# Hybrid attention and convolution block on one core: weighing V for four row tiles at once

## The chip, the cores and the metric

The kernel runs on one core of one Trainium2 chip. The metric is the device time of one execution in microseconds; lower is better. TensorE (PE) multiplies and transposes, VectorE (DVE) and ScalarE (ACT) work elementwise, GpSimd (POOL) clears small pieces of memory and issues a few DMAs, and SyncE (SP) issues nearly all DMAs.

## The reference

One layer: a normed input is projected to q, k, v, u and g; differential attention and a convolution branch run beside each other, are gated, merged and projected, and a SwiGLU follows. The change is in the attention alone (1024 tokens, 8 heads, v of 128 columns):

```python
def probs(qb, kf):
    s = jnp.einsum('bhqd,bhkd->bhqk', qb, kf) * scale + bias
    s = jnp.where(causal, s, -jnp.inf)
    return jax.nn.softmax(s, axis=-1)

p = probs(qb1, k1f) - lamf * probs(qb2, k2f)
return jnp.einsum('bhqk,bhkd->bhqd', p, vf)
...
a = rms_norm(a, subln_w[l]) * (1.0 - lam_init)
y_a = a.reshape(B, S, ATTN_WIDTH) @ w_proj_attn[l]
```

All of it is float32. Query row i sees keys up to i, so of the 8 x 8 tiles of 128 x 128 probabilities of a head, 36 are not zero.

## The kernel before, in words

Every float32 product is computed as three products of rounded parts (`mm3`, lines 171 to 173): high by high, high by low, low by high. `split_hi` (line 138, ScalarE) and `split_lo` (line 143, VectorE) make the parts.

The attention stage is a loop over 64 steps: 8 heads times 8 row tiles of 128 queries. Between its own matmuls stand those of the input projection that are still to be done (q, k and gate columns for later heads, tile `pg`), as filler for TensorE, and the taps of the depthwise convolution as filler for VectorE (tile `acc`, line 652).

For row tile i of head h a step does this:

- `scores(h, i)`: two score matmuls for each of the two softmaxes and each piece of up to 512 keys (tile `sc`, lines 1193 and 1194); VectorE adds the bias and finds the row bound (line 1195), ScalarE takes the exponential (line 1200), and VectorE joins both softmaxes into one unnormalised row (line 1209).
- `turn` of the step before: TensorE transposes its i + 1 probability tiles (`pT`, line 1229), and the two splits write them into `ph` and `pl`. These two tiles have one buffer each, with 8 key tiles of 256 query columns. So two row tiles fill one pair of tiles, the even one in columns 0 to 127, the odd one in 128 to 255. The even row tile has one key tile fewer than the odd one, and this hole is cleared by GpSimd (lines 1219 and 1220).
- `weigh`, after each odd row tile, in the same step as its `turn`: for each key tile up to the odd one's, three matmuls with a 128 x 128 tile of V as weights and 256 columns of `ph` or `pl` moving, all into one PSUM bank `pW`. With b = 0 to 3 these are 2, 4, 6 and 8 key tiles, 60 matmuls per head. ScalarE copies the result to `ar` (line 1243).
- `back`, two steps later: two transposes of `ar` (`pB`, line 1249), and for each row tile two ScalarE activations, one that scales and one that squares and sums (lines 1257 and 1258).
- After the last `back` of a head, `subln` scales its rows, and one step later `subln_T` transposes them (`pS`, line 1270), writes two tiles `at` (line 1272) and stores them in DRAM.

V of a head (`vh`, `vl`, one buffer each) is loaded after the last `weigh` of the head before.

`slot` runs what is due of `backs`, the late transposes of q and k (`pQ`, line 863), `sublns` and `weighs`, in this order and behind the projection work of the step. `slack_of` estimates how much longer TensorE takes than VectorE in each step, and the convolution's taps are dealt out by it. Three PSUM banks serve `pT`, `pW`, `pB`, `pS` and `pQ` in turn, three the scores, and two the projection. Within what the program fixes, the framework orders the instructions of each engine when the kernel is built, by a model of their times.

Of the kernel before, what the change touches and what calls it, by code (L numbers as in the profile page):

```python
# [10 lines left out]
F32 = mybir.dt.float32  # L11
F32R = mybir.dt.float32r
# [4 lines left out]
P = 128  # L17
S = 1024
D = 1024
H = 8  # L20
# [11 lines left out]
NT = S // P  # L32
# [43 lines left out]
def kernel(  # L76
# [28 lines left out]
    dve, act, pool, pe = nc.vector, nc.scalar, nc.gpsimd, nc.tensor  # L105
# [24 lines left out]
    def nm(s):  # L130
        uid[0] += 1
        return f"{s}_{uid[0]}"

    def f32(ap):
        return ap.bitcast(F32)

    def split_hi(dst, src):
        act.copy(dst, src)  # L138

    last_lo, last_mm = [None], [None]  # L140

    def split_lo(dst, src, hi):
        last_lo[0] = dve.tensor_tensor(dst, src, f32(hi), op=ALU.subtract).ins  # L143

    def after(ins):

        return nullcontext() if ins is None else tc.issue_after(ins)

    def last_of(engine):
        for ins in reversed(nc.cur_bb.bb.instructions):  # L150
            if ins.engine == engine:
                return ins
# [12 lines left out]
    def pm(z="pm"):  # L165
        npm[0] += 1
        p_, tag = pms[npm[0] % len(pms)]
        return p_.tile([P, 512], F32, tag=tag, name=nm(z))

    def mm3(o, lh, ll, rh, rl, start, stop):  # L170
        pe.matmul(o, lh, rh, start=start, stop=False)  # L171
        pe.matmul(o, lh, rl, start=False, stop=False)  # L172
        last_mm[0] = pe.matmul(o, ll, rh, start=False, stop=stop).ins  # L173
# [67 lines left out]
    at = [0]  # L241
# [884 lines left out]
    n = 0  # L1126
# [25 lines left out]
    aps = at_ctx.enter_context(tc.tile_pool(name="attn", bufs=2, reuse_waits="tile"))  # L1152
# [4 lines left out]
    V, TB, AN, SSA, PT, ES, RL = {}, {}, {}, {}, {}, {}, {}  # L1157

    def load_v(h):
        vh = aps.tile([P, NT, VD], F32R, tag="vh", name=f"vh{h}", bufs=1)  # L1160
        vl = aps.tile([P, NT, VD], F32R, tag="vl", name=f"vl{h}", bufs=1)
        for dst, src in ((vh, v_hi[h // 4]), (vl, v_lo[h // 4])):
            nc.sync.dma_start(
                f32(dst[:]),
                src[:, (h % 4) * VD : (h % 4 + 1) * VD].rearrange("(k p) d -> p k d", p=P),
            )
        V[h] = vh, vl

    def load_bias(h):
        tb = aps.tile([P, S], F32, tag="tb", name=f"tb{h}", bufs=1)  # L1170
        skew = t_d[h][:].rearrange("p l -> (p l)")[P - 1 : P - 1 + P * (TL - 1)]
        nc.sync.dma_start(tb[:], skew.rearrange("(p l) -> p l", l=TL - 1)[:, :S])
        TB[h] = tb

    def scores(h, i):
# [34 lines left out]
        dve.reciprocal(RL[h][:, i : i + 1], l[:, 0:1])  # L1210
        ES[h, i] = E[0]

    def turn(h, i):

        b = i // 2
        if (h, b) not in PT:
            ph = aps.tile([P, NT, 256], F32R, tag="ph", name=nm("ph"), bufs=1)
            pl = aps.tile([P, NT, 256], F32R, tag="pl", name=nm("pl"), bufs=1)
            pool.memset(f32(ph[:, 2 * b + 1, 0:P]), 0.0)
            pool.memset(f32(pl[:, 2 * b + 1, 0:P]), 0.0)  # L1220
            PT[h, b] = ph, pl
        ph, pl = PT[h, b]
        e = ES.pop((h, i))
        qs = slice((i % 2) * P, (i % 2 + 1) * P)
        for k0 in range(0, i + 1, 4):
            n = min(4, i + 1 - k0)
            pt = pm("pT")
            for k in range(n):
                pe.transpose(pt[:, k * P : (k + 1) * P], e[:, (k0 + k) * P : (k0 + k + 1) * P], ident[:])  # L1229
            src = pt[:, : n * P].rearrange("p (k q) -> p k q", q=P)  # L1230
            split_hi(ph[:, k0 : k0 + n, qs], src)
            split_lo(pl[:, k0 : k0 + n, qs], src, ph[:, k0 : k0 + n, qs])

    def weigh(h, b):

        ph, pl = PT.pop((h, b))
        vh, vl = V[h]
        o = pm("pW")
        nkt = 2 * b + 2
        for k in range(nkt):  # L1240
            mm3(o[:, :256], vh[:, k, :], vl[:, k, :], ph[:, k, :], pl[:, k, :], k == 0, k == nkt - 1)
        ar = aps.tile([P, 256], F32, tag="ar", name=nm("ar"), bufs=1)
        act.copy(ar[:], o[:, :256])
        return ar

    def back(h, b, ar):
        pt = pm("pB")
        for e in range(2):
            pe.transpose(pt[:, e * P : (e + 1) * P], ar[:, e * P : (e + 1) * P], ident[:])
        if h not in AN:  # L1250
            AN[h] = aps.tile([P, NT, VD], F32, tag="an", name=f"an{h}", bufs=1)
            SSA[h] = sm.tile([P, NT], F32, tag="ssa", name=nm("ssa"))
        jk = sm.tile([P, VD], F32, tag="jk", name=nm("jk"), bufs=1)
        for e in range(2):
            i = 2 * b + e
            src, r = pt[:, e * P : (e + 1) * P], RL[h][:, i : i + 1]
            act.activation(AN[h][:, i, :], src, AF.Identity, scale=r)
            act.activation(jk[:], src, AF.Square, scale=r, accum_out=SSA[h][:, i : i + 1])

    def subln(h):  # L1260
        an = AN[h]
        r = rstd_of(SSA[h][:], NT, 1.0 / VD, fast=True)
        dve.tensor_tensor(an[:], an[:], r.unsqueeze(2).to_broadcast([P, NT, VD]), op=ALU.mult)

    def subln_T(h):
        an = AN[h]
        for sb in range(2):
            pt = pm("pS")
            for i in range(4):
                pe.transpose(pt[:, i * P : (i + 1) * P], an[:, 4 * sb + i, :], ident[:])  # L1270
            at = aps.tile([P, 512], F32, tag="at", name=nm("at"), bufs=2)
            act.activation(at[:], pt[:], AF.Identity, scale=pcol("subln"))
            nc.sync.dma_start(a_d[h][:, sb * 512 : (sb + 1) * 512], at[:])
# [9 lines left out]
    scm, weighs, backs, sublns = [], [], [], []  # L1283
# [3 lines left out]
    def more(k):  # L1287

        with after(scm[-4] if len(scm) >= 4 else None):
            for _ in range(k):  # L1290
                next(fill, None)
        last_fill[0] = last_mm[0]
# [3 lines left out]
    def ready(queue, n):  # L1296
        now = [e for e in queue if e[0] <= n]
        queue[:] = [e for e in queue if e[0] > n]
        return [e[1] for e in now]

    def slot(n, nq):

        with after(last_fill[0]):
            for h, b, ar in ready(backs, n):
                back(h, b, ar)
                if b == NT // 2 - 1:
                    subln(h)
                    sublns.append((n + 1, h))
            for _ in range(nq):
                if late[0][0] <= n:  # L1310
                    late.pop(0)[1]()
            for h in ready(sublns, n):
                subln_T(h)
            for h, b in ready(weighs, n):
                backs.append((n + 2, (h, b, weigh(h, b))))
                if b == NT // 2 - 1 and h + 1 < H:
                    load_v(h + 1)

    def slack_of(h, i):

        p = (i + 1) * plan[h] // NT - i * plan[h] // NT
        nk = (i + 1) * P
        t_pe = nk * (2.52e-3 + (2.5e-3 if i % 2 else 0.0)) + 5.15 * p
        t_dve = 0.4 + 4.2e-3 * nk + p + 0.3
        return max(0.0, t_pe - t_dve)

# [5 lines left out]
    for n, (h, i) in enumerate(steps):  # L1332
        if i == 0:
            load_bias(h)
        p = (i + 1) * plan[h] // NT - i * plan[h] // NT
        nq = len(late)
        scores(h, i)
        scm.append(last_mm[0])
        more((p + 1) // 2)
        if n:  # L1340
            hp, ip = steps[n - 1]
            turn(hp, ip)
            if ip % 2:
                weighs.append((n, (hp, ip // 2)))
        more(p // 2)
        slot(n, nq)
        due += share * slack[n]
        with after(last_of(mybir.EngineType.DVE)):
            bg.step(int(due + 1e-6))
        due -= int(due + 1e-6)  # L1350
# [19 lines left out]
    def behind(*engines):  # L1370

        st = ExitStack()
        for e_ in engines:
            st.enter_context(after(last_of(e_)))
        return st

    hl, bl = H - 1, NT // 2 - 1
    with behind(E_.PE, E_.Activation, E_.DVE):
        wg = ws.next()
        with in_order(E_.PE):  # L1380
# [1 line left out]
    with after(last_mm[0]):  # L1382
        for h, b, ar in ready(backs, len(steps)):
            back(h, b, ar)
        ar = weigh(hl, bl)
# [40 lines left out]
    for h in KB:  # L1426
        for sb in range(2):
            cs = slice(sb * 512, (sb + 1) * 512)
            at = bp.tile([P, 512], F32, tag="ya", name=f"at{h}_{sb}", bufs=4)[:]
# [230 lines left out]
    o, part_ = {}, {}  # L1660
# [16 lines left out]
    for z, (a_, b_, s_, outs) in enumerate(YO):  # L1677
        start = s_ not in o
# [133 lines left out]
    o = {}  # L1812
    for z, (a_, b_, s_, (l, c), full) in enumerate(WO):
        if z == 6:
            h2_hi, h2_lo = Quad(big, "h2_hi", "xh"), Quad(big, "h2_lo", "xl")
        start = s_ not in o
        if start:
            o[s_] = [(pw if s_ == "c" else ps).tile([P, 512], F32, tag="pw" if s_ == "c" else PS_TAGS[i], name=nm("wo")) for i in range(4)]
        with in_order(mybir.EngineType.PE):
            for g in range(2):  # L1820
# [3 lines left out]
                for i in range(4):  # L1824
                    for k in range(2):
                        ah, al = a_part(a_, 2 * g + k, i)
                        for y_, (l_, r_) in enumerate(((ah, whi), (ah, wlo), (al, whi))):
                            last_mm[0] = pe.matmul(  # L1828
                                o[s_][i][:], l_, r_[:, k, :], start=start and g + k + y_ == 0,
                                stop=g == 1 and k == 1 and y_ == 2, skip_group_check=not start,  # L1830
# [3 lines left out]
        with in_order(mybir.EngineType.DVE, alone=True) if z == 5 else nullcontext():  # L1834
# [3 lines left out]
            for i in range(4):  # L1838
                t_ = 4 * l + i
                h = xa[t_][:, TOK[c]]  # L1840
# [322 lines left out]
```

## Time and profile before

| | |
|---|---|
| Median of 3 runs | 1722.73 us (1722.38 to 1724.52) |
| The profiled execution, time | 1722.03 us |
| Its span | 1720.0 us |
| Granted TensorE clock, mean | 1.0 |
| Attention stage, about | 320 to 825 us |
| Weighing matmuls (`pW`) | 480, first at 341.7 us, last at 817.7 us |

The profile gives the busy time of each engine, groups of instructions by line and shape, and single instructions with their start and duration. A row of the latter reads: start in us, duration in us, engine, line, operation, what is written from what, shape, count, and in brackets how long the engine had been idle and what released it. `PE` is the matmul itself, `PEld` the load of its weights, which runs beside other matmuls. The ends of matmuls are modelled; their starts are recorded.

### The profile page before, as it was taken

How to read it: one execution, taken by the hardware profiler on the slowest of the kernel's cores; microseconds unless marked ns; L12 is line 12 of the kernel's file. 1: busy time of each engine (PE TensorE's matmuls, PEld its weight loads, DVE VectorE, ACT ScalarE, POOL GpSimd, SP SyncE). 2: the span in 40 equal slices, each digit the busy share in tenths (PEclk: the TensorE clock that was granted, in tenths of full speed). 3: DMA queues.
4: the chain of work that ended last, by engine and by line, in shares of the span. 5: the costliest groups of instructions: out<-in, count | busy, mean ns of one | idle time of the engine just before them, and what ended most of it. 6: DMA issues, size and time to landing. Idle time of an engine off the chain costs nothing.

```text
span 1720.0 us, 25299 instructions
## 1 busy us (share of the span) xinstructions
PE 1711.1 (99%) x8882; PEld 1458.3 (85%) x8882; DVE 1334.0 (78%) x2275; ACT 822.5 (48%) x1926; POOL 27.2 (2%) x101
## 2 busy tenths in 40 slices
PE   9999999999999999999999999999999999999999
PEld 6878898999989998988888888888888888888887
DVE  8689988989988898987589797867776777555544
ACT  6121141558767686665557444853333333333332
POOL 0000000000000000000000000000000000000000
PEclk9999999999999999999999999999999999999999
DMA  7269544244444344355899565476756656687663
GB/s 246 87 202 314 183 127 127 70 123 129 112 125 131 116 117 132 108 147 163 295 323 321 183 238 199 159 246 208 227 188 206 189 184 191 203 287 241 216 215 128
DMA packets 286362, 318.57 MB, mean 185 GB/s; under 512 B 19106, under 2 KB 186067, under 8 KB 286236
## 3 DMA queue, kind: packets, MB, share of 16 engines
q1 hardware_dynamic: 283500, 307.07, 55.6%
q0 software_dynamic: 2432, 9.10, 2.2%
q8 instruction: 70, 1.15, 0.3%
q10 hardware_dynamic: 304, 0.79, 0.1%
q14 instruction: 56, 0.46, 0.1%
HBM read 204.91 MB, written 97.82 MB: 176 GB/s over the span
## 4 chain that ended last, share of the span: by engine, by line
PE 93%; DMA 2%; DVE 2%; ACT 2%; issue 0%; SPq 0%; ACTq 0%; DVEq 0%
PE acc L1875 20%; PE acc L578 12%; PE pg L171 12%; PE pg L172 12%; PE pg L173 11%; PE wo L1828 4%; PE yo L1671 4%; PE pg L779 4%; PE eg L1875 2%; PE sc L1194 2%; PE sc L1193 2%; PE pT L1229 2%; PE pW L171 1%; PE pW L173 1%; PE pW L172 1%; PE pQ L863 1%
## 5 line engine op out<-in xcount | busy, mean ns | idle before, releaser
L652 DVE SCALAR_TENSOR_TENSOR acc<-u,cw,acc 128x1024 f32<-128x1024 f32 x240 | 306.8, 1278 | 2.6
L171 PE MATMUL pg<-hT_hi,whi 128*128 128x512 f32 x512 | 201.7, 394 | 1.2 <-ACT sgg L688 0.9
L172 PE MATMUL pg<-hT_lo,whi 128*128 128x512 f32 x512 | 201.1, 393 | 0.0
L173 PE MATMUL pg<-hT_hi,wlo 128*128 128x512 f32 x512 | 200.8, 392 | 0.0
L138 ACT CAST whi<-wraw 128x1024 fp32r<-128x1024 f32 x106 | 111.7, 1053 | 158.4 <-PE pg L172 90.1
L143 DVE TENSOR_TENSOR wlo<-draw,whi 128x1024 fp32r<-128x1024 f32 x75 | 91.8, 1224 | 93.5 <-ACT whi L138 93.5
L143 DVE TENSOR_TENSOR wlo<-wraw,whi 128x1024 fp32r<-128x1024 f32 x107 | 130.5, 1220 | 42.3 <-ACT whi L138 41.8
L171 PE MATMUL pg<-whi,hT_hi 128*128 128x256 f32 x512 | 146.1, 285 | 0.3 <-ACT jk L847 0.3
L172 PE MATMUL pg<-wlo,hT_hi 128*128 128x256 f32 x512 | 145.7, 285 | 0.0
L173 PE MATMUL pg<-whi,hT_lo 128*128 128x256 f32 x512 | 145.3, 284 | 0.0
L138 ACT CAST whi<-draw 128x1024 fp32r<-128x1024 f32 x75 | 79.1, 1055 | 129.5 <-PE acc L578 126.0
L578 PE MATMUL acc<-wlo,whi 128*128 128x512 f32 x308 | 119.8, 389 | 0.0
L578 PE MATMUL acc<-whi,wlo 128*128 128x512 f32 x308 | 119.8, 389 | 0.0
L1200 ACT ACTIVATE E<-E,mn 128x256 f32<-128x256 f32 (+7 forms) x128 | 99.4, 778 | 33.0 <-DVE mn L1195 32.8
L171 PEld LDWEIGHTS pg<-hT_hi,whi 128*128 128x128 f32 x512 | 96.2, 188 | 21.3 <-ACT sgg L688 1.7
L172 PEld LDWEIGHTS pg<-hT_lo,whi 128*128 128x128 f32 x512 | 96.2, 188 | 19.3 <-issue 0.6
L173 PEld LDWEIGHTS pg<-hT_hi,wlo 128*128 128x128 f32 x512 | 96.2, 188 | 19.2
L171 PEld LDWEIGHTS pg<-whi,hT_hi 128*128 128x128 f32 x512 | 97.6, 191 | 1.9 <-ACT jk L847 0.5
L172 PEld LDWEIGHTS pg<-wlo,hT_hi 128*128 128x128 f32 x512 | 97.6, 191 | 1.5
L173 PEld LDWEIGHTS pg<-whi,hT_lo 128*128 128x128 f32 x512 | 97.6, 191 | 0.7
L1195 DVE CUSTOM_DVE_ANT_0 E<-sc,tb 128x512 f32<-128x512 f32 (+3 forms) x128 | 73.9, 586 | 17.3 <-PE sc L1194 6.3
L138 ACT CAST whi<-s 128x1024 fp32r<-128x1024 f32 x44 | 46.3, 1053 | 81.3 <-PE acc L1875 67.6
(392 smaller groups left out, 4285.8 us busy)
## 6 DMA issues: line engine op xcount, KB each, us to landing
wraw<-in_w_gate_up_dram SPq DMA_DIRECT2D x55, 512.0 KB, 5.7
wraw<-in_w_in_dram SPq DMA_DIRECT2D x37, 512.0 KB, 5.6
qs<-qs SPq DMA_DIRECT2D x96, 128.0 KB, 2.3
wd<-in_w_down_dram SPq DMA_DIRECT2D x44, 256.0 KB, 3.4
tdT<-wd SPq DMA_DIRECT2D x88, 128.0 KB, 4.2
draw<-sdS SPq DMA_DIRECT2D x44, 256.0 KB
draw<-tdT SPq DMA_DIRECT2D x44, 256.0 KB, 3.0
wraw<-in_w_in_dram SPq DMA_DIRECT2D x32, 256.0 KB, 4.6
```

The costliest lines, as they stand in the source:

```text
L138: act.copy(dst, src)
L143: last_lo[0] = dve.tensor_tensor(dst, src, f32(hi), op=ALU.subtract).ins
L171: pe.matmul(o, lh, rh, start=start, stop=False)
L172: pe.matmul(o, lh, rl, start=False, stop=False)
L173: last_mm[0] = pe.matmul(o, ll, rh, start=False, stop=stop).ins
L578: m = pe.matmul(o[s_][i][:], l_[:, ts], r_[:, 512:], start=start and j + y_ == 0, stop=j == n - 1 and y_ == 2, skip_group_check=not start,)
L652: dve.scalar_tensor_tensor(acc[0][:], us[c][:, t : t + S], cw[:, c, t : t + 1], acc[0][:], op0=ALU.mult, op1=ALU.add)
L779: last_mm[0] = pe.matmul(o[:], l_, r_, start=first and n_ == 0, stop=last and n_ == len(terms) - 1).ins
L1195: dve.tensor_tensor_reduce(e[:, ks], o[:, :w], tb[:, S - nk + c0 : S - nk + c0 + w], 1.0, mn[:, j : j + 1] if c0 else 3.0e38, ALU.add, ALU ...
L1200: act.activation(e[:, :nk], e[:, :nk], AF.Exp, bias=mn[:, j : j + 1], scale=-1.0, accum_out=l[:, j : j + 1])
L1671: last_mm[0] = pe.matmul(ob_[0][j][:], l_[:, j % 2, k, :], r_, start=start and k + y_ == 0, stop=k == 3 and y_ == 2, skip_group_check=not ...
L1875: last_mm[0] = pe.matmul(o[:], a_[x_][:, k, :], b_[y_][:, k, :], start=start and k + x_ + y_ == 0, stop=k == 3 and x_ == 1, skip_group_che ...
```

## The change

Row tiles 0 to 3 of a head become one group, which is weighed once, after row tile 3. Row tiles 4 and 5, and 6 and 7, stay pairs. The buffer of `ph` and of `pl` keeps its 2048 columns and is read as 4 key tiles of 512 query columns for the first group, and as 8 of 256 for the pairs. In the first group key tile k is multiplied only with the columns from 128 k on, since earlier queries don't see it: 512, 384, 256 and 128 columns. Nothing has to be cleared there. The low by high product of key tile 0 is moved to the end, so that the last matmul covers the whole bank. `ar` gets 512 columns and shares the two buffers of `at`. `back` turns four row tiles back together for the first group. The estimate in `slack_of` is adapted.

```diff
+    GROUPS = ((0, 4), (4, 2), (6, 2))
+
+    def group_of(i):
+        return max(0, i // 2 - 1)
+
     def turn(h, i):
 
-        b = i // 2
+        b = group_of(i)
+        q0, nq = GROUPS[b]
         if (h, b) not in PT:
-            ph = aps.tile([P, NT, 256], F32R, tag="ph", name=nm("ph"), bufs=1)
-            pl = aps.tile([P, NT, 256], F32R, tag="pl", name=nm("pl"), bufs=1)
-            pool.memset(f32(ph[:, 2 * b + 1, 0:P]), 0.0)
-            pool.memset(f32(pl[:, 2 * b + 1, 0:P]), 0.0)
-            PT[h, b] = ph, pl
+            PT[h, b] = [
+                aps.tile([P, NT * 256], F32R, tag=t_, name=nm(t_), bufs=1)[:].rearrange("p (k q) -> p k q", q=nq * P)
+                for t_ in ("ph", "pl")
+            ]
+            if b:
+                for t_ in PT[h, b]:
+                    pool.memset(f32(t_[:, q0 + 1, 0:P]), 0.0)
         ph, pl = PT[h, b]
         e = ES.pop((h, i))
-        qs = slice((i % 2) * P, (i % 2 + 1) * P)
+        qs = slice((i - q0) * P, (i - q0 + 1) * P)
...
         o = pm("pW")
-        nkt = 2 * b + 2
-        for k in range(nkt):
-            mm3(o[:, :256], vh[:, k, :], vl[:, k, :], ph[:, k, :], pl[:, k, :], k == 0, k == nkt - 1)
-        ar = aps.tile([P, 256], F32, tag="ar", name=nm("ar"), bufs=1)
-        act.copy(ar[:], o[:, :256])
+        q0, nq = GROUPS[b]
+        terms = [
+            (l_[:, k, :], r_[:, k, c0:], c0)
+            for k in range(q0 + nq) for c0 in [0 if b else k * P] for l_, r_ in ((vh, ph), (vh, pl), (vl, ph))
+        ]
+        if not b:
+            terms.append(terms.pop(2))
+        for n_, (l_, r_, c0) in enumerate(terms):
+            last_mm[0] = pe.matmul(
+                o[:, c0 : nq * P], l_, r_, start=n_ == 0, stop=n_ == len(terms) - 1, skip_group_check=c0 > 0
+            ).ins
+        ar = aps.tile([P, 512], F32, tag="at", name=nm("ar"), bufs=2)
+        act.copy(ar[:, : nq * P], o[:, : nq * P])
         return ar
 
     def back(h, b, ar):
         pt = pm("pB")
-        for e in range(2):
+        q0, nq = GROUPS[b]
+        for e in range(nq):
             pe.transpose(pt[:, e * P : (e + 1) * P], ar[:, e * P : (e + 1) * P], ident[:])
...
-        for e in range(2):
-            i = 2 * b + e
+        for e in range(nq):
+            i = q0 + e
...
     def slack_of(h, i):
 
         p = (i + 1) * plan[h] // NT - i * plan[h] // NT
         nk = (i + 1) * P
-        t_pe = nk * (2.52e-3 + (2.5e-3 if i % 2 else 0.0)) + 5.15 * p
+        t_pe = nk * (2.52e-3 + {3: 3.7e-3, 5: 2.5e-3, 7: 2.5e-3}.get(i, 0.0)) + 5.15 * p
...
-            if ip % 2:
-                weighs.append((n, (hp, ip // 2)))
+            if ip + 1 == sum(GROUPS[group_of(ip)]):
+                weighs.append((n, (hp, group_of(ip))))
```

The remaining lines replace `NT // 2 - 1`, the number of the last pair, by `len(GROUPS) - 1`.

More of the change, by code (lines that the diff above doesn't have):

```diff
@@ L1305, in slot @@
                 back(h, b, ar)
-                if b == NT // 2 - 1:
+                if b == len(GROUPS) - 1:
                     subln(h)
@@ L1315, in slot @@
                 backs.append((n + 2, (h, b, weigh(h, b))))
-                if b == NT // 2 - 1 and h + 1 < H:
+                if b == len(GROUPS) - 1 and h + 1 < H:
                     load_v(h + 1)
@@ L1375, in behind @@
         return st
-    hl, bl = H - 1, NT // 2 - 1
+    hl, bl = H - 1, len(GROUPS) - 1
     with behind(E_.PE, E_.Activation, E_.DVE):
```

## The prediction

> **What bounds the kernel now.** I read the head of the page and its first part, then a table of the stretch in which the edited code runs, then the chain of waits, and last the start times of single matmuls. The first part says which engine is full:
>
> ```profile
> span 1720.0 us, 25299 instructions
> PE 1711.1 (99%) x8882; PEld 1458.3 (85%) x8882; DVE 1334.0 (78%) x2275; ACT 822.5 (48%) x1926; POOL 27.2 (2%) x101
> ```
>
> The edited functions run only in the attention stage. The weighing matmuls (tile pW) start at 341.71 us and the last one before 818 us, so I took 320 to 825 us as one stretch (behind its length stand the busy time and the instructions of PE, PEld, DVE, ACT and POOL, then the granted clock, the DMA share and GB/s):
>
> ```profile
> 320.00:825.00 505.00, 503.06 (x3362) 459.49 (x3361) 434.48 (x1017) 341.51 (x1168) 15.09 (x68) 1.00 0.44 123
> ```
>
> TensorE is covered for 503.06 of 505.00 us at the full granted clock (1.00). VectorE has 70.5 us free, ScalarE 163.5. So here a microsecond taken from TensorE's own stream is a microsecond of time, as long as no other engine makes it wait. The chain that ended last agrees, with 93% of it on TensorE:
>
> ```profile
> PE 93%; DMA 2%; DVE 2%; ACT 2%; issue 0%; SPq 0%; ACTq 0%; DVEq 0%
> ```
>
> What a matmul costs cannot be read from its duration. The durations overlap: the next matmul starts long before the one before it has ended. In one weighing, undisturbed from the first row here to the last, nine matmuls start:
>
> ```profile
> 446.53 0.28 PE L171 MATMUL pW<-ph,vh 128*128 128x256 f32 x1
> ...
> 447.48 0.28 PE L173 MATMUL pW<-ph,vl 128*128 128x256 f32 x1
> ```
>
> That is 0.95 us for 8 steps, 0.119 us from start to start, while each row shows 0.28 us. The start-to-start step is the price on a full engine, and I use it throughout.
>
> **The change part by part.** *The weighing itself.* Per head the code before weighs four pairs of row tiles with 6, 12, 18 and 24 matmuls of 256 columns. The change replaces the first two (18 matmuls) by one weighing of 12: three each with 512, 384, 256 and 128 columns. The last two stay. Steps for the other widths, all from this stage:
>
> ```profile
> 468.12 0.40 PE L172 MATMUL pg<-hT_lo,whi 128*128 128x512 f32 x1
> ...
> 469.27 0.39 PE L171 MATMUL pg<-hT_hi,whi 128*128 128x512 f32 x1
> ...
> 440.02 0.34 PE L1193 MATMUL sc<-ks,qs 128*128 128x384 f32 x1
> 440.19 0.33 PE L1194 MATMUL sc<-ks,qs 128*128 128x384 f32 x1
> 440.37 0.28 PE L172 MATMUL pg<-wlo,hT_hi 128*128 128x256 f32 x1
> ```
>
> 512 columns: 1.15 us over 5 steps, 0.230 us. 384 columns: 0.35 over 2, 0.175 us. The 128-column ones need care, since a weight load of 128 columns goes with every matmul:
>
> ```profile
> 455.33 0.22 PE L1193 MATMUL sc<-ks,qs 128*128 128x128 f32 x1
> 455.39 0.28 PE L1194 MATMUL sc<-ks,qs 128*128 128x128 f32 x1
> 455.50 0.33 PE L171 MATMUL pg<-whi,hT_hi 128*128 128x256 f32 x1
> 455.67 0.28 PE L172 MATMUL pg<-wlo,hT_hi 128*128 128x256 f32 x1
> ```
> ```profile
> 455.22 0.19 PEld L1193 LDWEIGHTS sc<-ks,qs 128*128 128x128 f32 x1
> 455.34 0.19 PEld L1194 LDWEIGHTS sc<-ks,qs 128*128 128x128 f32 x1
> 455.44 0.19 PEld L171 LDWEIGHTS pg<-whi,hT_hi 128*128 128x128 f32 x1
> ```
>
> The first 128-column matmul is followed after 0.06 us, which looks like half the price of 256. But the next start comes after 0.11 and the one after that after 0.17: from 455.33 to 455.67 stand two of 128 and one of 256 columns, (0.34 - 0.119) / 2 = 0.11 us each. The loads show why: behind a 256-column matmul they start 0.12 us apart, behind the 128-column one still 0.10. A 128-column matmul is bound by the load of its successor. The transposes, also 128 columns each, say the same:
>
> ```profile
> 462.05 1.03 PE L863 MATMUL pQ<-ident,qkraw 128*128 128x128 f32 x8
> 462.84 0.36 PE L172 MATMUL pg<-wlo,hT_hi 128*128 128x256 f32 x1
> 463.04 0.28 PE L173 MATMUL pg<-whi,hT_lo 128*128 128x256 f32 x1
> ```
>
> From 462.05 to 463.04 stand eight of them and one 256-column matmul: (0.99 - 0.119) / 8 = 0.109 us.
>
> The sum per head: before, 18 x 0.119 = 2.142 us. After, 3 x (0.230 + 0.175 + 0.119 + 0.110) = 1.902 us. That is 0.240 us less, and over eight heads 1.92 us. A third of the instructions goes, but only a ninth of the time: the columns fall from 18 x 256 = 4608 to 3 x 1280 = 3840, and the 128-column third of the key tiles gives back part of it.
>
> Here the Trainium skill has a rule that speaks against the change: its page "TensorE: Matmul & The Clock Gate", section "LDWEIGHTS (loading the stationary operand)", puts a load at its columns divided by 1.2, about 107 ns for 128 columns. The trace agrees (0.109 and 0.11 us). The section "Back-to-back issue gap" of that page gives N / 2.4 + 2.5 ns for the matmul alone, about 56 ns at 128 columns; counted with 0.06 us, as the first step above would suggest, the saving would be 2.142 - 1.752 = 0.390 us per head, 3.1 us in all. The rows of the loads decide for the smaller sum.
>
> *Starting at a column inside a bank.* The shorter matmuls accumulate on the right part of the bank (columns 128, 256 and 384 on). The trace has no accumulation of this kind, but the eight transposes above write at such offsets, and at 0.109 us they take no more than the 128-column score matmuls (0.11), which start at the bank's first column. I take 0. As bounds I put the spread of these readings, 0.01 us, on the nine matmuls of a head that are concerned, to either side: 0.7 us.
>
> *Stalls at the removed weighings.* Three times in the stage TensorE stands before the first matmul of the first weighing of a head:
>
> ```profile
> 516.99 0.28 PE L172 MATMUL pg<-wlo,hT_hi 128*128 128x256 f32 x1
> 517.52 0.36 PE L171 MATMUL pW<-ph,vh 128*128 128x256 f32 x1 [0.25 <-DVE rl L1206]
> ...
> 585.22 0.28 PE L173 MATMUL pg<-whi,hT_lo 128*128 128x256 f32 x1
> 585.65 0.35 PE L171 MATMUL pW<-ph,vh 128*128 128x256 f32 x1 [0.16 <-ACT E L1200]
> ...
> 642.44 0.28 PE L171 MATMUL pg<-whi,hT_hi 128*128 128x256 f32 x1
> 642.93 0.36 PE L171 MATMUL pW<-ph,vh 128*128 128x256 f32 x1 [0.21 <-DMA vh<-v_hi]
> ```
>
> Steps of 0.53, 0.43 and 0.49 us where 0.119 is usual: 1.09 us lost. The first weighing now comes two row tiles later in the head. The load of V, which starts after the last weighing of the head before, has that much more time, so the third stall should go. The first two come from ScalarE and VectorE running late with the exponentials, and this lateness stays and may show at the next weighing. Bounds 0 and 1.09; I take half, 0.5 us gained.
>
> *The way back.* The four transposes of a group's result come together, and behind them eight ScalarE activations instead of two times four. For one pair they hold ScalarE from the first row here to the second, 1.20 us:
>
> ```profile
> 441.93 0.37 ACT L1257 ACTIVATE an<-pB,rl 128x128 f32<-128x128 f32 x1 [0.22 <-PE pB L1249]
> ...
> 443.13 0.52 ACT L1200 ACTIVATE E<-E,mn 128x256 f32<-128x256 f32 x1
> ```
>
> Their count stays 64; what is new is that the queue behind them waits 2.4 us once instead of 1.2 us twice. Queued there are the evictions of the projection's banks (sgg, qkraw), and those release TensorE. It has happened once at full size in the 32 bursts of the kernel before:
>
> ```profile
> 472.91 0.34 PE L1194 MATMUL sc<-ks,qs 128*128 128x384 f32 x1
> 474.00 0.51 PE L171 MATMUL pg<-hT_hi,whi 128*128 128x512 f32 x1 [0.76 <-ACT sgg L688]
> ```
>
> 1.09 us instead of 0.175: 0.92 us lost. Eight bursts of double length: 8 / 32 x 2 x 0.92 = 0.46, so I take 0.5 us lost. The bounds are 0 and one more pair's time in each head, 8 x 1.20 = 9.6 us.
>
> *The rest, with one answer each.* The evictions of pW go from 16 of 256 columns to 8 of 512 for these rows, and a 512-column one takes 0.688 us (the "at" row below): at most 8 x 0.688 = 5.5 us more if the 16 cost nothing, nothing if two small ones cost as much; off the path with 163.5 us free on ScalarE: 0. The result tile now shares two buffers with "at", so the first eviction of a head waits for the store of "at" to DRAM, issued a row tile earlier:
>
> ```profile
> L1272 ACT ACTIVATE at<-pS,pvec x14: 681/688/702, 409.2 to 778.8; 128x512 f32<-128x512 f32 x14
> ...
> DMA to landing us min/median/max: 2.0/2.7/3.4
> ```
>
> A row tile lasts 505 / 64 = 7.9 us on average, so 3.4 us are covered: 0. If that cover failed, the eviction, then ScalarE's queue, would wait up to 3.4 us. GpSimd drops 16 of 64 memsets; it is busy 15.09 us of 505, and what is queued behind them there (its DMAs and the memsets of the convolution's rows) can only come earlier: 0. Transposes into the probability tiles, the splits, the V loads and SyncE's queue keep their instructions. The new slack table moves a convolution tap from one row tile to another in some heads; VectorE has 70.5 us of room: 0 on average.
>
> Sum: -1.92 - 0.5 + 0.5 = -1.9 us. The profiled execution took 1722.03 us, 2.03 outside its span, and would take 1720.1. The median of the runs, 1722.73, lies 0.70 above it: 1720.8 us, 0.11% faster. The runs shown spread by 2.14 us, so 0.2%, 3.4 us, is about what a measurement can tell from no change.
>
> **The rivals.**
>
> *All three stalls go and nothing new comes* (chance 0.25). Then -1.92 - 1.09 = -3.0, and and, with other stalls lost in the redrawn order, more: the 0.92 us quoted at 472.91 gone too, it would be -3.9 us. 1718.8 to 1719.7. For it: fewer weighings, 24 instead of 32, each a place where TensorE meets the late engines. Against: the lateness itself is not removed.
>
> *The return burst becomes the bound* (chance 0.10, the other sign). Mechanism and place: eight activations behind the first group's transposes, two row tiles later, while TensorE needs a projection bank evicted. Price 1.20 us a head beyond now. With 1.9 us saved it costs time from the second head on, and passes the 0.2% at (3.4 + 1.9) / 1.2, five heads of eight; in all eight, 1722.73 - 1.9 + 9.6 = 1730.4 us. For it: the step at 472.91. Against: that happened in one of 32 bursts, and ScalarE is busy 341.51 of 505 us.
>
> *The order is drawn anew and gives the saving back* (chance 0.17). The instructions are ordered when the kernel is built, so every gap can move. The four stalls quoted make 2.0 us; as much again elsewhere gives 1722.73 - 1.9 + 2.0, about 1722.8, and 1725 with twice that. Not measurable.
>
> *The durations are the price* (chance 0.03). By the shown durations in the rows above (0.28 us at 256 columns, 0.40 at 512, 0.33 at 384, 0.28 for the second one of 128) the saving is larger: 18 x 0.28 - 3 x (0.40 + 0.33 + 0.28 + 0.28) = 1.17 us a head, 9.4 us, and the median 1713.4. Against it: nine matmuls of 0.28 us stand in 1.23 us of the first rows quoted.
>
> **How the numbers follow.** The forecast itself (between 1719.3 and 1722.0 us) gets 0.45. Faster by over 0.2% means below 1719.3: about all of the durations case, most of the first rival and a little of the forecast's edge, 0.28. Slower by over 0.2% means above 1726.2: the burst, and a tail of the redrawn order, 0.12. The rest, 0.60, is within. The range runs from 1717, where every gap quoted is gone (-1.92 - 1.09 - 0.92) and 1.8 us for gaps not quoted, to 1725.5, the redrawn order at twice its price; it leaves out the burst in most heads and the durations case, and a tail.
>
> **What would show it.** In the changed kernel, 96 first-group matmuls in place of 144, their steps 0.23, 0.175, 0.119 and 0.11 us, a 128-column one not at 0.06. The first group's twelve take 1.9 us where nothing breaks in. TensorE's share of the stage still 99%, the stage some 2 us shorter. Stalls named vh<-v_hi gone. The return of a group as one run of 2.4 us on ScalarE, and behind it sgg or qkraw as releasers of pg; if these grow past 2 us in total, the prediction is wrong towards slower. It is wrong towards faster if steps at the other weighings also close up.

## The result, and the profile after

The median went from 1722.56 to 1716.43 us (6 runs each): 6.1 us less, ratio 0.9965, 95% interval 0.9952 to 0.9978. On a second chip the same kernel took 1716.75 us beside 1721.82 for the kernel before, ratio 0.9974 (0.9963 to 0.9984), 5.1 us less. The forecast was 1720.8 us, 1.9 less, with 1717 as the lower end. The direction held. The size did not.

First the head and the first part of the page of the changed kernel, and its attention stage as one stretch (length, then busy time and instructions of PE, PEld, DVE, ACT, POOL, then clock, DMA share and GB/s):

```profile
span 1714.6 us, 25140 instructions
...
PE 1706.8 (100%) x8834; PEld 1455.0 (85%) x8834; DVE 1331.8 (78%) x2275; ACT 822.3 (48%) x1918; POOL 21.6 (1%) x69
```
```profile
320.00:821.00 501.00, 499.55 (x3315) 456.55 (x3314) 433.34 (x1017) 342.46 (x1160) 9.89 (x38) 1.00 0.44 124
```

TensorE has 48 matmuls less (8834 against 8882), 6 in each head, and is covered for 499.55 of 501 us. VectorE and ScalarE do what they did. So TensorE still bounds the stage, and the question is only what the 5.4 us were by which the span is shorter.

Now the first weighing of head 3, in a stretch of PE's timeline where nothing breaks in (it follows transposes, which makes its first step 0.32 instead of 0.23 us):

```profile
531.35 0.48 PE L1255 MATMUL pW<-ph,vh 128*128 128x512 f32 x1
531.67 0.39 PE L1255 MATMUL pW<-pl,vh 128*128 128x512 f32 x1
...
532.77 0.22 PE L1255 MATMUL pW<-ph,vh 128*128 128x128 f32 x1
532.83 0.28 PE L1255 MATMUL pW<-pl,vh 128*128 128x128 f32 x1
532.94 0.55 PE L1255 MATMUL pW<-ph,vl 128*128 128x128 f32 x2
533.34 0.27 PE L173 MATMUL pg<-whi,hT_lo 128*128 128x256 f32 x1
```

From 531.35 to 533.34 are 1.99 us, less the 0.09 of the first step 1.90 us for the twelve; the prediction had 1.902. The first 128-column matmul is again followed after 0.06 us and the next after 0.11. (The last row of `pW` merges two matmuls: the third one of 128 columns and, behind it, the moved one of 512.)

**A ledger of TensorE's time.** I took every start-to-start step of the stage, from the first score matmul to the last `pS` transpose, and split it into the usual step of its width (0.229, 0.174, 0.120 and 0.108 us for 512, 384, 256 and 128 columns, within 0.002 us of the medians of these traces) and the rest, which I call standing. It is a sum over some 3460 rows of the trace, not a view of the profile. A line of usual steps is a count of matmuls times these four prices, so two kernels with the same matmuls have the same sum there. Both kernels were profiled twice:

| us | before | before, again | changed | changed, again |
|---|---|---|---|---|
| attention stage | 521.95 | 521.19 | 517.63 | 517.09 |
| of it usual steps | 516.73 | 516.73 | 514.59 | 514.59 |
| of it standing | 5.22 | 4.46 | 3.04 | 2.50 |
| behind the stage, to the last matmul's start | 881.21 | 880.71 | 880.39 | 880.61 |
| span | 1720.0 | 1719.3 | 1714.6 | 1714.3 |

On the means of the two profiles, of 5.2 us in the span 2.1 are narrower work, 2.1 are standing, 0.5 lie behind the stage, where TensorE's instructions are the same and only six of them, near 842 us, change places, and the rest lies at the edges of these stretches.

Where the kernel before stood longest, at 472.91 us, its ScalarE row (timeline of ScalarE) shows the gate bank's eviction inside the first pair's way back. The changed kernel has no such first pair:

```profile
473.00 0.37 ACT L1257 ACTIVATE an<-pB,rl 128x128 f32<-128x128 f32 x1
473.25 0.70 ACT L688 ACTIVATE sgg<-pg,pvec 128x512 f32<-128x512 f32 x1
```

The changed kernel's longest stands are elsewhere, at scores and transposes (timeline of PE, the row before and the row that waited; a third, of 0.53 us at 448.05, waits for VectorE's joined row):

```profile
620.10 0.28 PE L172 MATMUL pg<-wlo,hT_hi 128*128 128x256 f32 x1
620.82 0.33 PE L1193 MATMUL sc<-ks,qs 128*128 128x128 f32 x1 [0.44 <-DMA ks<-klo]
...
744.89 0.49 PE L1237 MATMUL pT<-ident,E 128*128 128x128 f32 x3
745.90 0.30 PE L1193 MATMUL sc<-ks,qs 128*128 128x128 f32 x1 [0.52 <-DMA ks<-klo]
```

Both wait for the parts of k at a head's first scores. At 745 us TensorE is there 5 us earlier than in the kernel before, while the last transfer of k was issued only 3.9 us earlier. At 620 us the last transfer of k was itself issued 3.15 us later than in the kernel before, though TensorE came earlier; why SyncE issued it so late stays open (timeline of SyncE, first the kernel before, then the changed one):

```profile
614.68 0.55 SPq L884 DMA_DIRECT2D ks<-klo  x1
```
```profile
617.83 0.46 SPq L884 DMA_DIRECT2D ks<-klo  x1
```

### The profile page after: what moved, and what is told of

It reads as the page before. It is cut to its first block, busy times and chain, and to the rows that moved or that the text cites. A ratio compares the mean times of both kernels' runs of the same rounds, so it can differ in the third digit from the quotient of the medians.

```text
span 1714.6 us, 25140 instructions
## 1 busy us (share of the span) xinstructions
PE 1706.8 (100%) x8834; PEld 1455.0 (85%) x8834; DVE 1331.8 (78%) x2275; ACT 822.3 (48%) x1918; POOL 21.6 (1%) x69
## 4 chain that ended last, share of the span: by engine, by line
PE 95%; DMA 2%; DVE 1%; ACT 1%; issue 0%; SPq 0%; ACTq 0%
PE acc L1892 21%; PE acc L578 12%; PE pg L171 12%; PE pg L172 12%; PE pg L173 12%; PE wo L1845 4%; PE yo L1688 4%; PE pg L779 4%; PE eg L1892 4%; PE pW L1255 3%; PE sc L1194 2%; PE sc L1193 2%; PE pT L1237 2%; DMA xt<-in_x_dram 1%; PE pQ L863 1%; PE tr L1798 0%
## 5 line engine op out<-in xcount | busy, mean ns | idle before, releaser
L578 PE MATMUL acc<-whi 128*128 128x512 f32 x308 | 84.6, 389 | 0.0
```

Source lines behind the costliest of these rows:

```text
L578: m = pe.matmul(o[s_][i][:], l_[:, ts], r_[:, 512:], start=start and j + y_ == 0, stop=j == n - 1 and y_ == 2, skip_group_check=not start,)
```

## The experiments

Theory 1: 1.9 us are narrower work, and the rest is standing saved by weighing once and later. Theory 2: the rest is the luck of an order drawn anew when the kernel is built. Theory 3: the number of matmuls counts by their durations.

**The group, weighed as pairs (`e1_pairs_late`).**

```diff
-        terms = [...]                       # 512, 384, 256, 128 columns
+        for c0, nkt in ((0, 2), (256, 4)) if not b else ((0, q0 + nq),):
+            cs = slice(c0, c0 + 256)
+            for k in range(nkt):
+                mm3(o[:, cs], vh[:, k, :], vl[:, k, :], ph[:, k, cs], pl[:, k, cs], k == 0, k == nkt - 1)
```

(and the two holes cleared by GpSimd)

> The changed kernel with its first group weighed as two pairs again, but at the late place and with the joint way back: 18 matmuls of 256 columns (6 for row tiles 0 and 1, 12 for 2 and 3) in the layout of 512 query columns, with the two holes cleared by GpSimd. Theory 1 (the gain is 1.9 us of narrower work, and the rest is standing time of TensorE saved by weighing once and later): the 1.9 us come back, 1718.3 us, still 4 us under the kernel before, and the stage holds some 3 us of standing time, not 5. Theory 2 (the rest is the luck of an order drawn anew): the time can lie anywhere between 1716 and 1725 us, with standing time moved to other places. Theory 3 (the number of matmuls counts, by their durations): 6 matmuls a head of 0.28 us come back, and the time is about 1726 us.

Measured: 1720.0 us against 1722.34 (0.9989, 0.9980 to 0.9998). The counted steps are those of the kernel before, 516.73 us, and 4.09 us are standing. That the work came back can be seen without the counting: from each of the group's matmuls to the next start of any, the trace has 17.4 us over the eight heads, in the changed kernel 15.4. Of the changed kernel's lead over the kernel before, these 2 us of narrower work are gone, and 1.3 more, since the standing is longer than in either profile of the changed kernel (4.09 against 2.77 on average). Theory 3 (1726) is out. Between the other two this run doesn't decide.

**Full columns (`e2_full_cols`).**

```diff
-            for k in range(q0 + nq) for c0 in [0 if b else k * P] for l_, r_ in (...)
+            for k in range(q0 + nq) for c0 in [0] for l_, r_ in (...)
```

(and the unseen columns cleared by GpSimd)

> The changed kernel with all twelve matmuls of the first group at 512 columns; the columns that earlier queries don't see are cleared by GpSimd (three stretches per tile) and multiplied as zeros. By the start-to-start steps each head pays 12 x 0.230 - 1.902 = 0.86 us more, 6.9 us in all: 1723.3 us, about the kernel before. Theory 3 (durations: 12 x 0.40 against 3 x (0.40 + 0.33 + 0.28 + 0.28)) says 0.93 us a head, 7.4 us, 1723.8 us; so here only theory 2 (the order) differs, which allows 3 us to either side.

Measured: 1724.99 us (1.0020, 1.0011 to 1.0029). The counted steps are 521.43 us, 6.84 more than in the changed kernel, and the measured ones behind the group's matmuls agree: 22.2 us over the eight heads against 15.4, 6.8 more, where 6.9 were expected. The rest is again standing, 4.34 us. Its longest place is the late k: at 627.38 us the first score matmul of head 5 has lost 1.6 us, and the last transfer of k had been issued at 623.86.

**The slack tables exchanged (`e3_before_new_slack`, `e4_after_old_slack`).**

```diff
-        t_pe = nk * (2.52e-3 + (2.5e-3 if i % 2 else 0.0)) + 5.15 * p
+        t_pe = nk * (2.52e-3 + {3: 3.7e-3, 5: 2.5e-3, 7: 2.5e-3}.get(i, 0.0)) + 5.15 * p
```

(this in the kernel before, its reverse in the changed kernel)

> The kernel before with the slack table of the changed one, nothing else: a few taps of the convolution move by one row tile, and the order is drawn anew. Theory 1: within 0.7 us of the kernel before, 1722.6 us, and about 5 us of standing time in the attention stage as before. Theory 2: it moves by 2 us or more in either direction, as the changed kernel's unexplained part did. A rival inside theory 1, that the new dealing of taps brought the gain: 1719 to 1720 us.

> The changed kernel with the slack table of the kernel before, nothing else. Theory 1: 1716.4 us, within 0.7 us. Theory 2: moved by 2 us or more in either direction. That the dealing of taps brought the gain: 1719 to 1720 us.

Measured: 1724.16 us (1.0013, 1.0004 to 1.0022), standing 6.25; and 1718.62 us (0.9980, 0.9971 to 0.9988), standing 3.73. With the other's table the kernel before is 1.8 us slower. The changed one leads the kernel before by 3.7 us instead of 5.1 to 6.1, but the intervals overlap, so its loss is not clear of noise. The first outcome doesn't fit "within 0.7 us". An edit that changes no work moves the standing by about 1 us. That the new table alone brought the gain is excluded: in the kernel before it costs, and without it the changed kernel keeps 3.7 us.

**Both once more (`e5_after_again`, `e6_before_again`).**

> The changed kernel once more, unedited, for a second profile and a time on the chip of the runs beside it. Every theory: within 0.1% of 1716.4 us, 1714.7 to 1718.1. Its standing time of TensorE in the attention stage (start-to-start beyond the usual step) should be 3.0 us within some 0.3, since the order is the same, and the part behind the attention, which was 0.8 us shorter than in the kernel before with the same instructions, shows by how much that part varies by itself.

> The kernel before once more, unedited, for a second profile. Every theory: 1722.5 us within 0.1%. Standing time in the attention stage 5.2 us within 0.3 if the order sets it; if it comes out near 4, the 2.2 us that the changed kernel saved there are chance between executions.

Measured: 1716.75 and 1722.1 us; the profiles are in the ledger. The standing of one order repeats within 0.8 us in the kernel before and 0.54 in the changed one, so neither repeats within the 0.3 expected. The second profile of the kernel before has 4.46 us, between the two readings that its text offered. The stands at the gate bank (0.92 and 0.35 us) and behind `pB` (0.46) came again to 0.01 us. The three before the first weighings, on which I had set a term, did not: none of the three first matmuls stood over 0.1 us this time (at the third weighing the wait for `vl` behind the first matmul, 0.25 us, came again). So these depend on the execution.

**The kernel before with a late way back (`e7_before_back_late`), and its control (`e10_before_shared_at`).** The control has the first two lines only.

```diff
-        ar = aps.tile([P, 256], F32, tag="ar", name=nm("ar"), bufs=1)
+        ar = aps.tile([P, 512], F32, tag="at", name=nm("ar"), bufs=2)
...
-                backs.append((n + 2, (h, b, weigh(h, b))))
+                backs.append((n + (2 if b else 4), (h, b, weigh(h, b))))
```

> The kernel before with one thing moved: the way back of the first pair (two transposes, four activations) waits two row tiles more and comes together with that of the second pair, as in the changed kernel; the result tile shares the two buffers of at, so that both can be held. All weighings stay where and as they were. Theory 1, made more exact by the traces (two evictions of a gate bank, sgg, stood inside the first pair's four activations and held TensorE for 0.92 and 0.35 us; the change removes this burst from that place): these two stalls go, 1.3 us less than the kernel before, 1721.1 us, and the stalls before the first weighings (1.3 us) stay. Theory 2 (an order drawn anew): 2 us in either direction. If the longer burst of eight activations is what costs, as the prediction had it: slower than the kernel before, by 0.5 to 4 us.

> The kernel before with its result tile in the two buffers of at (as the changed kernel has it, and as in the run with the late way back), nothing else moved. If that run was faster because the first pair's activations left their place, this one stays at the kernel before, 1722 us, with the two stalls of 0.92 and 0.35 us behind the gate bank's eviction still there. If the shared buffers or an order drawn anew brought it, this one is faster too, 1720 to 1721 us.

Measured: with the late way back 1720.33 us against 1721.82 (0.9992, 0.9983 to 1.0001), standing 3.04, of which 0.85 before `pg` (2.2 in the kernel before). The interval of the time includes no change. The control, on another chip, 1726.64 us against 1721.83 (1.0031, 1.0019 to 1.0043): standing 9.40 us. Neither part of what was expected came. The two stands at the gate bank are gone though the activations were not moved, and three new ones cost more than 4 us (timeline of PE, the longest, from the control):

```profile
611.34 0.28 PE L171 MATMUL pg<-whi,hT_hi 128*128 128x256 f32 x1
613.36 0.39 PE L172 MATMUL pg<-wlo,hT_hi 128*128 128x256 f32 x1 [1.75 <-DVE wlo L143]
```

A weight tile's low part was made too late for the projection. The other two are at the scores, at 636.57 us (for the parts of q) and at 638.22 (for VectorE's split into `pl`). Nor is the control a mere redrawing of the order: in four places ScalarE waits, 7.0 us in all, to write `at` until the store of `at` has landed, and in the run with the late way back it waits so too (7.7 us with `ar`). Neither the kernel before nor the changed one has such a wait. One of these waits, at 414.69 us, lies just ahead of a stand of 0.52 us at 416.64; none lies near the three long ones.

So the run with the late way back cannot be put down to the moved burst alone. The order counts for more than I had allowed.

**The way back in halves (`e8_back_halves`).**

```diff
-                backs.append((n + 2, (h, b, weigh(h, b))))
+                ar = weigh(h, b)
+                if b:
+                    backs.append((n + 2, (h, b, ar)))
+                else:
+                    backs.extend([(n + 2, (h, b, ar, (0, 1))), (n + 3, (h, b, ar, (2, 3)))])
```

> The changed kernel with the way back of the first group cut in two: row tiles 0 and 1 where all four were, 2 and 3 one row tile later, so that no burst is longer than four activations. If the burst of eight costs what the prediction put on it (0.5 us), the time falls to 1715.9 us; if the burst costs nothing, 1716.4 us. Theory 2: 2 us in either direction. If four bursts per head are worse than three whatever their length, 1717 to 1718 us.

Measured: 1718.07 us against 1721.82 (0.9979, 0.9970 to 0.9988), 1.3 us over the unedited changed kernel beside it. Standing 3.91 us, 1.65 of it in one stand, in the last weighing of head 0:

```profile
385.65 0.40 PE L1194 MATMUL sc<-ks,qs 128*128 128x512 f32 x1
387.54 0.39 PE L1255 MATMUL pW<-ph,vh 128*128 128x256 f32 x1 [1.49 <-ACT jk L1276]
```

This stand lies behind the way back of row tiles 4 and 5, not behind one of the halves; the second half now comes one row tile ahead of it, and whether that delays it is not shown. So shorter bursts gained nothing. A burst of eight is there in the changed kernel (timeline of ScalarE, first row, and the exponential that follows the last):

```profile
668.36 0.37 ACT L1274 ACTIVATE an<-pB,rl 128x128 f32<-128x128 f32 x1
...
670.75 1.20 ACT L1200 ACTIVATE E<-E,mn 128x1024 f32<-128x1024 f32 x1
```

It takes 2.39 us, as estimated, but it is the only one of eight that runs unbroken. In the other seven heads exponentials or evictions stand between the eight activations, and at 487 us a gate bank's eviction too. No stand of TensorE over 0.15 us lies behind any of the eight.

**The last key tile at 256 columns (`e9_last_256`).**

```diff
-            for k in range(q0 + nq) for c0 in [0 if b else k * P] for l_, r_ in (...)
+            for k in range(q0 + nq) for c0 in [0 if b else min(k * P, 2 * P)] for l_, r_ in (...)
```

(and the hole cleared by GpSimd)

> The changed kernel with the last key tile of the first group at 256 columns instead of 128; the hole is cleared by GpSimd. If a 128-column matmul is held by the next weight load (0.11 us from start to start, against 0.119 at 256 columns), 24 matmuls pay 0.01 us more: 0.2 us, and the usual steps of the attention stage sum to the same within 0.3 us. If it cost 0.06 us, they would pay 1.4 us more. The time as a whole, 1717 us, can move by 1 to 1.5 us with the order drawn anew, as the slack table's edit moved it, so the steps decide and not the time.

Measured: 1715.83 us against 1721.83 (0.9968, 0.9956 to 0.9979), not to be told from the changed kernel. The same weighing of head 3, from its first row to the first behind it:

```profile
531.13 0.48 PE L1257 MATMUL pW<-ph,vh 128*128 128x512 f32 x1
...
533.14 0.28 PE L173 MATMUL pg<-whi,hT_lo 128*128 128x256 f32 x1
```

2.01 us against 1.99: three matmuls of twice the columns cost 0.02 us more in all. Over the eight heads it is 15.6 us against 15.4, 0.23 more, where 0.2 were expected, and 1.4 if 128 columns cost 0.06 us. A 128-column matmul is worth 0.11 us here, not 0.06. The profiled execution of this kernel stood 3.0 us once behind the attention (PE waits for DVE, tile u), and took 1720.71 us; the median of 1715.83 doesn't have that.

**Four edits that only redraw the order, each in both kernels.** The edits: the slack table's constant, its price per key, its price of a filler piece, and the larger half of an odd number of filler pieces behind the transposes.

```diff
-        t_dve = 0.4 + 4.2e-3 * nk + p + 0.3
+        t_dve = 1.2 + 4.2e-3 * nk + p + 0.3     # n1
+        t_dve = 0.4 + 3.4e-3 * nk + p + 0.3     # n2
...
-        more((p + 1) // 2)                      # n3: ahead of turn; the other half behind it
+        more(p // 2)
...
-        t_pe = ... + 5.15 * p
+        t_pe = ... + 4.4 * p                    # n4
```

> The kernel before with one constant of the slack table raised (VectorE's share of a step 0.8 us longer): no work changes, some taps are dealt to other row tiles, and the order is drawn anew. Its partner is the changed kernel with the same edit. Theory 1 (weighing late and once saves standing time whatever the order): the partner stands 2 us less in the attention stage, and is 4 us faster. Theory 2 (the order's luck): both stand somewhere between 2 and 9 us with no fixed sign, and the times differ by 2.1 us plus that.

> The changed kernel with the same constant raised. Theory 1: standing time near 3.5 us, 2 us less than its partner. Theory 2: anywhere between 2 and 9 us.

> The kernel before with the slack table's VectorE time per key lowered by a fifth: only the dealing of taps and so the order changes. Theory 1: about 5 us of standing time, 2 us more than the partner. Theory 2: no fixed sign.

> The changed kernel with the slack table's VectorE time per key lowered by a fifth. Theory 1: about 3.5 us of standing time, 2 us less than the partner. Theory 2: no fixed sign.

> The kernel before with the projection's filler dealt differently within a step (where the number of pieces is odd, the larger half comes behind the transposes instead of ahead of them). No work changes. Theory 1: standing time about 2 us more than in the partner. Theory 2: no fixed sign, and 2 to 9 us in either kernel.

> The changed kernel with the filler dealt in that way. Theory 1: about 2 us less standing time than the partner, and 4 us faster. Theory 2: no fixed sign.

> The kernel before with the slack table's price of a filler piece lowered from 5.15 to 4.4 us: only the dealing of taps and the order change. Theory 1: about 5 us of standing time, 2 us more than the partner. Theory 2: no fixed sign.

> The changed kernel with the slack table's price of a filler piece lowered from 5.15 to 4.4 us. Theory 1: about 3.5 us of standing time, 2 us less than the partner. Theory 2: no fixed sign.

Measured, in us, beside the unedited kernels (second chip; standing is the mean of their two profiles; beside the redrawn ones the kernel before took 1722.02 us for n1 and n2, 1721.96 for n3 and n4). "Pairs" is the kernel before, "group" the changed one:

| | median pairs, group | standing pairs, group | before pg | before pW | before sc and pT |
|---|---|---|---|---|---|
| unedited | 1721.82, 1716.75 | 4.84, 2.77 | 2.23, 0.39 | 1.53, -0.10 | 0.43, 2.01 |
| n1 | 1721.49, 1717.16 | 3.96, 3.17 | 1.63, 0.30 | 1.15, 0.06 | 0.41, 2.40 |
| n2 | 1721.28, 1718.89 | 4.41, 5.15 | 1.79, 0.52 | 1.10, -0.09 | 0.93, 2.84 |
| n3 | 1722.27, 1716.21 | 4.05, 2.40 | 1.84, 0.18 | 0.43, 0.42 | 0.94, 0.70 |
| n4 | 1721.18, 1716.96 | 3.64, 2.74 | 1.64, 0.24 | 0.81, 0.05 | 0.43, 2.04 |

The group is faster in all five, by 2.4 to 6.1 us, 4.4 on average. It stands less in four of five, by 0.9 us on average, not 2. Inside this small sum two larger ones hide. The stands before the projection's banks go in every pair (1.83 to 0.33 us on average), those before weighings in all but n3, where they stay (1.00 to 0.07), and those before scores and transposes come in four of five (0.63 to 2.00). Neither theory is right as put: part of the saving belongs to the change, and the order adds or takes 1 to 2 us. The 0.9 us of all standing are not clear of chance, since the five differences run from -0.7 to 2.1 us; the fall before the projection's banks is clear, 1.3 to 1.8 us in every pair.

## Why the prediction was right or wrong

- **The price by start-to-start steps** held: 1.902 us predicted for a group, 1.90 seen, and 2.1 us in the ledger against 1.92 in the sum. The 0.2 between them is rounding of the steps (0.119 and 0.11 in the prediction, 0.120 and 0.108 in the medians, over 144 matmuls before and 96 after). With the last key tile at 256 columns a head became 0.02 to 0.03 us dearer; at 0.06 us for 128 columns it would have been 0.18. By that the section "LDWEIGHTS (loading the stationary operand)" of the page "TensorE: Matmul & The Clock Gate" of the Trainium skill, about 107 ns for 128 columns, agrees with the trace, 108 ns. (The prediction's "128-column third of the key tiles" is a quarter, one of four; its sum counts them rightly.)
- **Columns inside a bank at no cost** held: the steps in the rows above are the usual ones.
- **"Stalls at the removed weighings", half of 1.09 us,** was the wrong size. Stands before weighings fell by 0.9 us on average over the five pairs, and by 1.6 between the unedited kernels. But the three rows on which I set it did not repeat in the same kernel, so the sign came right on weak evidence, partly by luck.
- **"The way back", 0.5 us lost,** is the step that failed in sign: where it put 0.5 us more, the stands before `pg` fell by 1.5 us on average, 1.8 between the unedited kernels. I priced one unbroken burst of eight, and the order breaks it up in seven of eight heads; nothing over 0.15 us stands behind any. And I forgot that the first pair's burst leaves its own place. In two heads of the kernel before it stood where TensorE also asks for a gate bank. A stand over 0.15 us behind a gate bank is in six of the eight profiles of kernels that bring the first pair back early, and in none of the twelve that bring it back late. That the burst's leaving is the cause is likely but not shown: in the control and in the kernel before with n3 the gate-bank stands are gone though the burst stays, and the saving of n3 before `pg` lies in other stands.
- **What I left out:** the stands before scores and transposes, 1.4 us more on average. I had written that the engines' lateness "stays and may show at the next weighing"; it showed at the scores and transposes instead. With the two terms above this makes -0.9 - 1.5 + 1.4 = -1.0, about the -0.9 of the five pairs (the rest is before other tiles).
- **The shared buffers at 0** held in the changed kernel, where ScalarE never waits for a store of `at`. In the control it does, up to 2.6 us at a time, within the 3.4 us that the prediction gave as the bound.
- **The rivals.** The burst as the bound is excluded by the result, and the durations by it and by `e1_pairs_late`. "All three stalls go" came nearest: the stand at 472.91 us, its condition for -3.9 us, went too. But new stands came, against its name, and its 1718.8 us is still 2.4 us above the result. The redrawn order was given a chance only of taking the saving back; it can give too. Edits that change no work moved the kernel before by +1.8 us (the other's slack table) and -0.8 to +0.3 (n1 to n4), and the changed one by +2.1 at most (n2); the control's +4.8 holds waits of its own. So luck of either sign, some 1 to 2 us, is in the measured 5.1 to 6.1 us, and the lower end, 1717, allowed for less than all these terms together.
- **GpSimd's memsets** fall from 64 to 32, not by 16: two pairs per head lose two each. No run here shows what that is worth by itself.
- **Open:** of the 4.4 us by which the five pairs differ, 2.1 are narrower work and 0.9 standing; some 1.4 lie outside the stage's ledger, behind it or at the edges, where the instructions are the same, or in the difference between a profiled execution and the median. Single executions differ behind the stage by as much (880.4 to 882.1 us over the eight profiles of the redrawn kernels), so I can't say whether it is real.

No kernel here is shown to beat the changed one: n3 in the group (0.9967 of the kernel before) and the last key tile at 256 columns (0.9968) lie beside its 0.9965 and 0.9974.

## What to carry to other kernels

On a full TensorE, price an edit by the steps from start to start, with a floor at the load of the next weights; narrowing a matmul below 256 columns bought almost nothing here. When an edit takes a piece of work out of a place, cost the waits at that place too, not only those at the new one. And where an edit can redraw the instruction order when the kernel is built, measure a few edits that change no work, in both kernels, before you explain the last 2 us of a difference.

## What I had not expected of the hardware

A 128-column matmul followed by another starts its successor after 0.06 us, and gives it back: the one after that waits 0.11 us and the next 0.17 when it has 256 columns. Measured over a closed stretch, 128 columns cost 0.11 us and 256 cost 0.12. And the same instruction stream stands within 0.8 us of itself from one execution to the next, with some stands repeating to 0.01 us (0.92 and 0.93 at the gate bank), while others come and go: the three before the first weighings, and one of 0.68 us at a score matmul that waited for a DMA.
